# Vector arithmetic moved from GpSimd to VectorE in an encoder layer, with earlier first forms and a third early pair

## The chip, the cores and the metric

The kernel runs on one core of one Trainium2 chip. The metric is device time in microseconds (us). The core's engines work side by side, each through its own instruction stream in program order: TensorE (PE; its weight loads are shown as PEld), VectorE (DVE), ScalarE (ACT), GpSimd (POOL) and SyncE (SP). SP only issues DMAs; POOL issues some too. Engines wait for each other through semaphores.

## The reference

One layer of an encoder in float32: 512 tokens, model width 2048.

```python
h = rms_norm(x, g_mix_pre)
proj = h @ w_in                                   # 2048 x 6144
out_a = diff_attention(...)                       # heads 0 to 7
out_b = stick_breaking(...)                       # heads 8 to 15
mix = concatenate([out_a, out_b]) @ w_out         # 2048 x 2048
x = x + rms_norm(mix, g_mix_post)
h = rms_norm(x, g_mem_pre)
o = memory_attention(h, mem_n, w_mq, w_mkv, w_mo) # 4 heads, 256 memory tokens
x = x + rms_norm(o, g_mem_post)
h = rms_norm(x, g_ffn_pre)
gu = h @ w_gate_up                                # 2048 x 11264
f = (silu(gu[..., :D_FF]) * gu[..., D_FF:]) @ w_down
x = x + rms_norm(f, g_ffn_post)
```

## The kernel before, in words

**Precision.** A float32 product is made of three PE matmuls on parts: each operand is split into a rounded part h (a cast on ACT) and the rest l = x - h (a subtraction on DVE), and PE sums h*h, h*l and l*h. A weight of 128x1024 (512 KB) is split by `Weights.split`: L127 is the cast on ACT, L128 the subtraction on DVE. A 128x512 piece of activations is split by `split` (L236 cast, L237 subtraction). PE's matmuls nearly all come from the helper `mm` (L233).

**Weights.** All weights pass in one fixed list of chunks. `Weights.load` issues them on SP (L116) as slots come free: five slots `raws`, with three more (`mraw`, later `raw`) at some places. Some chunks are sums of two blocks of a weight. Those are made by a second, accumulating DMA that POOL issues: onto a fresh load (L118), or onto a slot whose chunk is already split (L136, "add"). Some are summed on DVE (L133). Two weights ahead of the one in use are split.

**Products.** The out-projection (`w_out`) and the FFN (`w_gu`, `w_dn`) are block products with seven products in place of eight, in class `Blocks`: columns in pairs of 512, tokens in two halves. Product i takes a *form* of the activations (a quarter, or a sum or difference of quarters, split in h and l) and a chunk for each of 4 blocks; it is 4 x 12 = 48 matmuls of 512 columns for a pair of columns. Forms are stored in quarters of the large tile `big`, or in tiles of their own. `evict` then adds the product in PSUM to what is held (L912, L973, L980; L1006 and L1007 for product 7 when it came before 6).

**Stages.** Cross-attention keys and values; 16 heads (0 to 7 differential, 8 to 15 stick-breaking), each with its projection; out-projection; cross-attention; FFN. Stick-breaking is a chain through ACT (e, sph, w, sqh), DVE and PE. Its results, with those of the other heads, are `mix`. The out-projection first makes product 1 and product 7 of both pairs (`EARLY`, from heads 0 to 7 alone), then 2, 3, 5, 6, 4 of each pair. After it, each of four token blocks t has a `chain`: residual (L844), transposes on PE (L854) and splits. Beside it PE folds the memory keys into `w_mq` (`fold_keys`). In the FFN products 1 and 2 of the first two column pairs are made *early*, before the forms of 5, 3, 6, 7 and 4 are needed (`late_forms`); L861 is the scaling of a transposed token block ahead of them.

**What sets the order.** Work that is to run beside PE's matmuls is written as generators in two queues, `side` and `side2`. `fill`, called behind every few matmuls, steps both: a generator yields an integer (so many steps) or a float (so many us of matmuls) to wait. A scheduler then orders each engine's instructions; an instruction that is pinned (`pin`, keep in program order) can't be moved ahead of its predecessor on its engine.

**What the change touches.** `sub_p` (L909) is a subtraction of 128x512 on POOL: 16 of them for the out-projection's forms (`mix_forms`), 16 for `late_forms`. L1006 and L1007 are 8 sums on POOL, L1079 a gain, on DVE for tokens of the first half and on POOL (8 times) for the second. `mix_form(1, 0)` makes the first form of product 1 once all heads are written down; the other three follow in `mix_forms` with `big` as home.

Of the kernel before, what the change touches and what calls it, by code (L numbers as in the profile page):

```python
# [36 lines left out]
NF = 12  # L37
NQ = 8
TW = 640

# [151 lines left out]
def encoder_kernel(ctx: ExitStack, tc: tile.TileContext, a: dict, out: bass.AP):  # L192
# [114 lines left out]
    for cb in range(NCB):  # L307
        wm("w_mo", cb, range(8))
    for j, cbs in enumerate(gu_cbs[:2]):
        wf("w_gu", cbs, 0, 4, ORDER[:2], MAKE)  # L310
    for j, cbs in enumerate(gu_cbs):
        wf("w_gu", cbs, 0, 4, ORDER[2 if j < 2 else 0 :], MAKE, j == 1)
    for b, n in enumerate(DOWN):
# [410 lines left out]
    def sb_gen(h, q, k, v):  # L724
# [52 lines left out]
        yield from subnorm(o, h, gains[:, G_SB : G_SB + 1])  # L777

    for g in range(4):
        v = v_block(g)  # L780
        for h in range(4 * g, 4 * g + 4):
            cq, ck = qk_cts(h)
            scale = 64 ** -0.5 if h < HD else 128 ** -0.5
            if h + 1 < HD:
                spread_bias(h + 1)
            q = proj_hl("w_qk", cq, scale)
            k = proj_hl("w_qk", ck, 1.0)
            side.add((diff_gen if h < HD else sb_gen)(h, q, k, v))


# [3 lines left out]
    class Sub:  # L794
# [78 lines left out]

        def chain(self, t):
            ss2 = yield from self.residual(t, True)
            yield CH[0]
            for cb in range(NCB):
                self.turn(t, cb)
                if cb == NCB - 1:
                    s2, r2 = st(), st()  # L880
                    nc.vector.tensor_reduce(s2, ss2, axis=AX.X, op=ALU.add)
                    pow_rstd(r2, s2, 1)
                    self.r2[t] = r2
                yield CH[1]
# [22 lines left out]

    def sub_p(o, x, y):
        nc.gpsimd.tensor_tensor(o, x, y, op=ALU.subtract)  # L909

    def sub2(o, x, y):
        nc.vector.tensor_tensor(o, x, y, op=ALU.subtract)  # L912

    class Blocks:
# [55 lines left out]
        def evict(self, i, t, p):  # L970
# [17 lines left out]
            elif i == 6:  # L988
# [13 lines left out]
                if (7, t) in T:  # L1002
                    w = T.pop((7, t))

                    def last():
                        nc.gpsimd.tensor_tensor(v, v, w, op=ALU.add)  # L1006
                        nc.gpsimd.tensor_tensor(r, r, w, op=ALU.add)  # L1007

# [14 lines left out]

    mixforms = {}

    def mix_form(i, k2, src, loose=False):
        if i in HOMES_MIX and not loose:
            a_, b_ = HOMES_MIX[i]
            k = 8 * a_ + 2 * k2
            h, l = (big[:, x, k : k + 2, b_ * M : (b_ + 1) * M] for x in range(2))  # L1030
        else:
            h, l = u2(s="mixh"), u2(s="mixl")
        split(h, l, src)
        mixforms[i, k2] = (h, l)

    def mix_forms():

        for k2 in range(1, 4):
            mix_form(1, k2, mix[k2, 0])
            yield 2  # L1040
        for k2 in range(4):
            t = u2(F32, "s7")
            sub_p(t, mix[k2, 1], mix[k2, 0])
            mix_form(7, k2, t)
            yield 2
        for k2 in range(4):
# [3 lines left out]
            mix_form(2, k2, a12)  # L1050
            sub_p(a21, a21, a22)
            yield 1
            sub_p(a11, a11, a21)
            yield 1
            sub_p(a12, a12, a11)
            late_mix[k2] = (a12, a21, a11, a22)
            yield 1
# [3 lines left out]
            yield 1  # L1061
        for n, i in enumerate((5, 6, 4)):
            for k2 in range(4):
                while (7, 1) not in done_mix:
                    yield 0
                mix_form(i, k2, late_mix[k2][1 + n])
                yield 2.0
# [6 lines left out]
    def mix_done(cbs):  # L1074
        def done(t, nh, c):
            cb = cbs[nh]
            sub.mark = c
            nc.scalar.activation(junk, c, AF.Square, accum_out=sub.ss[t][:, cb : cb + 1])
            (nc.vector if t < 2 else nc.gpsimd).tensor_tensor(c, c, sub.g[cb], op=ALU.mult)  # L1079
            sub.y[t, cb] = c  # L1080
            if cb == col_pairs[-1][t < 2]:
                (side, side2)[t // 2].add(sub.chain(t))
        return done
# [4 lines left out]

    mix_form(1, 0, mix[0, 0], True)
    side2.add(mix_forms())  # L1090
# [100 lines left out]
    for pair in range(2):  # L1191
        for r in range(KT):
            fold_keys(pair, r)
        if pair == 0:
            side2.add(load_keys(1))
        else:
            side2.add(load_values([0], True))
# [79 lines left out]
    def early_forms(t):  # L1277
        while not fv_done:
            yield 0
        for i, g0 in ((1, 0), (2, 2)):  # L1280
            for g in range(2):
                form(i, g, t, h3[g0 + g, t])
                yield 0

    def late_forms(t):
        for g in range(2):
            a11, a12, a21, a22 = (h3[g + 2 * c, t + 2 * r] for r in range(2) for c in range(2))
            s = u(s="s")
            sub_p(s, a21, a22)
            form(5, g, t, s)  # L1290
            yield 0
            sub_p(a21, a21, a11)
            form(7, g, t, a21)
            yield 0
            sub_p(s, a11, s)
            form(6, g, t, s)
            yield 0
            sub_p(a12, a12, s)
            form(3, g, t, a12)
            yield 0  # L1300
            form(4, g, t, a22)
            yield 0

# [155 lines left out]

    early = [Blocks("w_gu", cbs, 0, 4, gated(j)) for j, cbs in enumerate(gu_cbs[:2])]  # L1460
    for g in early:
# [7 lines left out]
    for j, cbs in enumerate(gu_cbs):  # L1469
        g = early[j] if j < 2 else Blocks("w_gu", cbs, 0, 4, gated(j))  # L1470
        past = set()
        if j == NFB - 1:
            side2.add(block_forms(0, past))
        for i in ORDER[2 if j < 2 else 0 :]:
            g.product(i)
# [146 lines left out]
```

## Time and profile before

| | us |
|---|---|
| runs of before: median (lowest, highest) of 3 | 2753.44 (2747.07, 2760.84) |
| the profiled execution | 2757.57 |
| its span, from first to last instruction | 2755.4 |
| POOL's subtractions at L909 (32), busy | 55.1 |
| POOL's powers of 128x1 at L388 (20), busy | 17.3 |

The profile is of one execution. A page gives busy time by engine, the span in 40 slices, and the costliest groups of instructions; a trace answers further questions: who waited for whom, instructions in order of time, and busy times by stretch. "Granted clock" is the share of full speed at which TensorE was let run.

### The profile page before, as it was taken

How to read it: one execution, taken by the hardware profiler on the slowest of the kernel's cores; microseconds unless marked ns; L12 is line 12 of the kernel's file. 1: busy time of each engine (PE TensorE's matmuls, PEld its weight loads, DVE VectorE, ACT ScalarE, POOL GpSimd, SP SyncE). 2: the span in 40 equal slices, each digit the busy share in tenths (PEclk: the TensorE clock that was granted, in tenths of full speed). 3: DMA queues.
4: the chain of work that ended last, by engine and by line, in shares of the span. 5: the costliest groups of instructions: out<-in, count | busy, mean ns of one | idle time of the engine just before them, and what ended most of it. 6: DMA issues, size and time to landing. Idle time of an engine off the chain costs nothing.

```text
span 2755.4 us, 33701 instructions
## 1 busy us (share of the span) xinstructions
PE 2663.9 (97%) x12608; PEld 2205.2 (80%) x12608; DVE 1717.0 (62%) x2329; ACT 1322.9 (48%) x1936; POOL 336.0 (12%) x345
## 2 busy tenths in 40 slices
PE   8999999999997998999998999999999999999996
PEld 7888877888886778888886888888888888878775
DVE  5673555554456779335467655555555568787887
ACT  5542444455455546334445444444444456454553
POOL 0000000000003132000015221111211221102101
PEclk9999999999998999999999999999999999999998
DMA  8882222222225776233556998888989889878776
GB/s 287 294 266 97 81 92 84 82 87 76 77 74 148 188 194 215 78 122 106 163 174 149 249 216 206 203 202 203 203 202 207 198 221 252 222 248 202 199 205 204
DMA packets 166021, 480.64 MB, mean 174 GB/s; under 512 B 18529, under 2 KB 29177, under 8 KB 165857
## 3 DMA queue, kind: packets, MB, share of 16 engines
q1 hardware_dynamic: 127776, 344.37, 37.1%
q0 software_dynamic: 38080, 134.12, 26.5%
q8 instruction: 98, 1.61, 0.2%
q14 instruction: 67, 0.54, 0.1%
HBM read 441.70 MB, written 39.34 MB: 175 GB/s over the span
## 4 chain that ended last, share of the span: by engine, by line
PE 82%; DMA 5%; issue 5%; DVE 5%; ACT 1%; POOL 1%; SPq 0%; POOLq 0%; ACTq 0%; DVEq 0%
PE ps L233 80%; DVE parts L128 2%; DMA raws<-in_w_dn_dram 1%; DMA xres<-x_d 1%; DMA mraw<-in_w_out_dram 1%; ACT parts L127 1%; PE ps L1368 1%; DMA kraw<-kT_d 1%; DVE big L237 1%; DMA actT_d<-fT 0%; POOL y_d L1488 0%; DMA raw<-in_w_dn_dram 0%; DMA xnat<-in_x_dram 0%; PE ps L854 0%; DVE form L237 0%
## 5 line engine op out<-in xcount | busy, mean ns | idle before, releaser
L233 PE MATMUL ps<-parts,big 128*128 128x512 f32 x4824 | 1141.0, 394 | 38.2 <-DVE parts L128 24.1
L233 PEld LDWEIGHTS ps<-parts,big 128*128 128x128 f32 x4824 | 907.2, 189 | 239.6 <-DVE parts L128 33.9
L128 DVE TENSOR_TENSOR parts<-raws,parts 128x1024 fp32r<-128x1024 f32 x555 | 686.9, 1240 | 572.7 <-ACT parts L127 567.6
L127 ACT CAST parts<-raws 128x1024 fp32r<-128x1024 f32 x555 | 583.1, 1052 | 704.3 <-PE ps L233 628.6
L233 PE MATMUL ps<-parts,form 128*128 128x512 f32 x2376 | 552.3, 390 | 2.9 <-ACT parts L127 2.7
L233 PEld LDWEIGHTS ps<-parts,form 128*128 128x128 f32 x2376 | 444.7, 188 | 97.7 <-ACT parts L127 4.8
L233 PE MATMUL ps<-big,parts 128*128 128x512 f32 x1536 | 375.2, 394 | 0.0
L233 PEld LDWEIGHTS ps<-big,parts 128*128 128x128 f32 x1536 | 282.7, 188 | 61.4 <-issue 3.9
L128 DVE TENSOR_TENSOR parts<-raw,parts 128x1024 fp32r<-128x1024 f32 x175 | 216.1, 1238 | 154.7 <-ACT parts L127 154.4
L127 ACT CAST parts<-raw 128x1024 fp32r<-128x1024 f32 x175 | 183.9, 1054 | 197.2 <-PE ps L233 161.0
L136 POOL DMA_DIRECT2D raws<-in_w_gu_dram x112 | 97.8, 873 | 823.2 <-DVE parts L128 622.8
L233 PE MATMUL ps<-memhl,parts 128*128 128x512 f32 (+1 forms) x1024 | 184.0, 341 | 10.4 <-DVE memhl L244 8.8
L233 PEld LDWEIGHTS ps<-memhl,parts 128*128 128x128 f32 x1024 | 158.1, 190 | 35.6 <-DVE memhl L244 8.8
L233 PE MATMUL ps<-khl,parts 128*128 128x256 f32 x768 | 99.3, 289 | 0.0
L233 PEld LDWEIGHTS ps<-khl,parts 128*128 128x128 f32 x768 | 95.5, 195 | 0.2
L118 POOL DMA_DIRECT2D raws<-in_w_out_dram x12 | 11.0, 920 | 686.0 <-DMA raws<-in_w_out_dram 680.1
L233 PE MATMUL ps<-big,pTh 128*128 128x512 f32 x256 | 80.1, 392 | 0.0
L233 PE MATMUL ps<-gh,big 128*128 128x512 f32 x256 | 79.1, 389 | 0.0
L136 POOL DMA_DIRECT2D raw<-in_w_gu_dram x60 | 52.4, 873 | 111.6 <-DVE parts L128 108.4
L688 ACT ACTIVATE e<-e,small 128x512 f32<-128x512 f32 (+3 forms) x64 | 35.4, 555 | 51.9 <-DVE small L686 51.9
L136 POOL DMA_DIRECT2D raws<-in_w_dn_dram x30 | 26.2, 875 | 256.5 <-DVE parts L128 203.8
L233 PEld LDWEIGHTS ps<-gh,big 128*128 128x128 f32 x256 | 48.1, 188 | 10.0
(964 smaller groups left out, 2381.3 us busy)
## 6 DMA issues: line engine op xcount, KB each, us to landing
raws<-in_w_gu_dram POOLq DMA_DIRECT2D x113, 512.0 KB, 6.7
raws<-in_w_gu_dram SPq DMA_DIRECT2D x79, 512.0 KB, 4.4
raws<-in_w_qk_dram SPq DMA_DIRECT2D x64, 512.0 KB, 3.3
raw<-in_w_gu_dram POOLq DMA_DIRECT2D x63, 512.0 KB, 6.8
raw<-in_w_gu_dram SPq DMA_DIRECT2D x57, 512.0 KB, 3.7
aq<-actT_d SPq DMA_DIRECT2D x82, 256.0 KB, 6.0
raws<-in_w_dn_dram SPq DMA_DIRECT2D x41, 512.0 KB, 5.4
raws<-in_w_mk_dram SPq DMA_DIRECT2D x32, 512.0 KB, 5.1
```

The source lines that it names most:

```text
L118: self.nc.gpsimd.dma_start(t[0], x, accum_op=ALU.add)
L127: self.nc.scalar.copy(h, r)
L128: self.nc.vector.tensor_tensor(l, r, h.bitcast(F32), op=ALU.subtract)
L136: self.nc.gpsimd.dma_start(r, self.chunks[m][3], accum_op=ALU.add)
L233: nc.tensor.matmul(o, l, r, start=start, stop=stop, skip_group_check=True)
L237: pin(nc.vector.tensor_tensor(l, src, h.bitcast(F32), op=ALU.subtract))
L688: nc.scalar.activation(es[m][:, 0:n], es[m][:, 0:n], AF.Exp, bias=nmx[:, m : m + 1], accum_out=z[:, m : m + 1],)
L1368: nc.tensor.transpose(tp[:, k * P : (k + 1) * P], f[:, k * P : (k + 1) * P], ident)
```

## The change

All tile arithmetic of `sub_p`, L1006, L1007 and L1079 is issued on VectorE. The two 128x512 adds of the last residual (L842) and the small powers stay on GpSimd. The first form of the out-projection is made for all four blocks by a generator that is queued with head 12, one piece per 12 us of matmuls, in tiles of its own. Forms of the out-projection and the FFN, and the subtractions ahead of them, are pinned. In `mix_forms` form 5 moves up to the first loop. The chains of token blocks 2 and 3 wait for 12 us of matmuls first. `load_keys(1)` goes to the other queue. A third column pair of the FFN has its products 1 and 2 early; the chunk of its product 5 is then loaded anew (four chunks) rather than summed in place.

```diff
+NE = 3
...
-    for j, cbs in enumerate(gu_cbs[:2]):
+    for cbs in gu_cbs[:NE]:
         wf("w_gu", cbs, 0, 4, ORDER[:2], MAKE)
     for j, cbs in enumerate(gu_cbs):
-        wf("w_gu", cbs, 0, 4, ORDER[2 if j < 2 else 0 :], MAKE, j == 1)
+        wf("w_gu", cbs, 0, 4, ORDER[2 if j < NE else 0 :], MAKE, 0 < j < NE)
...
+    def mix_form(i, k2, src, loose=False):
+        if i in HOMES_MIX and not loose:
...
+        split(h, l, src, pin)
+        mixforms[i, k2] = (h, l)
+
+    def first_forms():
+
+        for k2 in range(4):
+            mix_form(1, k2, mix[k2, 0], True)
+            yield 12.0
+
     for g in range(4):
...
+            if h == 12:
+                side2.add(first_forms())
...
-        def chain(self, t):
+        def chain(self, t, wait=0.0):
+            yield wait
...
-    def sub_p(o, x, y):
-        nc.gpsimd.tensor_tensor(o, x, y, op=ALU.subtract)
-
     def sub2(o, x, y):
-        nc.vector.tensor_tensor(o, x, y, op=ALU.subtract)
+        return nc.vector.tensor_tensor(o, x, y, op=ALU.subtract)
...
-                        nc.gpsimd.tensor_tensor(v, v, w, op=ALU.add)
-                        nc.gpsimd.tensor_tensor(r, r, w, op=ALU.add)
+                        add(v, v, w)
+                        add(r, r, w)
...
     def mix_forms():
-        for k2 in range(1, 4):
-            mix_form(1, k2, mix[k2, 0])
-            yield 2
         for k2 in range(4):
             t = u2(F32, "s7")
-            sub_p(t, mix[k2, 1], mix[k2, 0])
+            pin(sub2(t, mix[k2, 1], mix[k2, 0]))
             mix_form(7, k2, t)
...
             mix_form(3, k2, a12)
             yield 1
-        for n, i in enumerate((5, 6, 4)):
+            mix_form(5, k2, a21)
+            yield 1
+        for n, i in enumerate((6, 4)):
...
-            (nc.vector if t < 2 else nc.gpsimd).tensor_tensor(c, c, sub.g[cb], op=ALU.mult)
+            nc.vector.tensor_tensor(c, c, sub.g[cb], op=ALU.mult)
             sub.y[t, cb] = c
             if cb == col_pairs[-1][t < 2]:
-                (side, side2)[t // 2].add(sub.chain(t))
+                (side, side2)[t // 2].add(sub.chain(t, 12.0 * (t > 1)))
...
-    mix_form(1, 0, mix[0, 0], True)
+    side2.drain()
     side2.add(mix_forms())
...
-            side2.add(load_keys(1))
+            side.add(load_keys(1))
...
     def late_forms(t):
...
-            sub_p(s, a21, a22)
-            form(5, g, t, s)
-            yield 0
+            pin(sub2(s, a21, a22))
+            form(5, g, t, s, 4, pin)
+            yield 3.0
...
-    early = [Blocks("w_gu", cbs, 0, 4, gated(j)) for j, cbs in enumerate(gu_cbs[:2])]
+    early = [Blocks("w_gu", cbs, 0, 4, gated(j)) for j, cbs in enumerate(gu_cbs[:NE])]
```

How it moves instructions, at three places. First POOL, from the loads of the out-projection on (`mix` and `s` are the operands of the forms, `raws` and `mraw` the weights' slots). Before:

```order
L118 DMA raws<-in_w_out_dram 128x1024 x5
L909 TENSOR_TENSOR s_816_6704<-mix_2460,mix_2458 128x512
L909 TENSOR_TENSOR s_820_6745<-mix_3111,mix_3109 128x512
L909 TENSOR_TENSOR mix_2460<-mix_2460,mix_5026 128x512
L909 TENSOR_TENSOR mix_3111<-mix_3111,mix_5562 128x512
L118 DMA raws<-in_w_out_dram 128x1024
L909 TENSOR_TENSOR mix_2458<-mix_2458,mix_2460 128x512
```

Of the change:

```order
L120 DMA raws<-in_w_out_dram 128x1024 x9
L120 DMA mraw_7041<-in_w_out_dram 128x1024
L120 DMA mraw_7042<-in_w_out_dram 128x1024
L120 DMA raws<-in_w_out_dram 128x1024
L138 DMA raws<-in_w_out_dram 128x1024 x3
```

POOL's stream there holds accumulating loads alone; the subtractions that stood between them are gone from it.

Second PE, in the stick-breaking chain of head 14 (`sph`, `spl` are its two parts, `mixh`, `mixl` those of product 1's form). Before:

```order
L233 MATMUL ps_6445<-spl_6474,nones_r 128x256
L233 MATMUL ps_6444<-sph_6482,ntri_r 128x384
L233 MATMUL ps_6444<-sph_6473,nones_r 128x256 x2
L233 MATMUL ps_6444<-spl_6483,ntri_r 128x384
L233 MATMUL ps_6444<-spl_6474,nones_r 128x256 x2
L233 MATMUL ps_6443<-sph_6491,ntri_r 128x512
```

Of the change:

```order
L235 MATMUL ps_6461<-spl_6490,nones_r 128x256
L235 MATMUL ps_6568<-parts,mixh_5912 128x512 x2
L235 MATMUL ps_6568<-parts,mixl_5913 128x512
L235 MATMUL ps_6569<-parts,mixh_5912 128x512 x2
L235 MATMUL ps_6569<-parts,mixl_5913 128x512
L235 MATMUL ps_6568<-parts,mixh_5912 128x512
L235 MATMUL ps_6460<-sph_6498,ntri_r 128x384
L235 MATMUL ps_6460<-sph_6489,nones_r 128x256 x2
L235 MATMUL ps_6460<-spl_6499,ntri_r 128x384
```

Matmuls of product 1 now stand between the steps of the chain: 7 here, 22 ahead of the step of 128x512.

Third DVE, while the late forms of the FFN are made (`h` and `s` are the operands, `form` and `big` the results, `parts` the weights). Before:

```order
L128 TENSOR_TENSOR parts<-raw_10876,parts 128x1024
L237 TENSOR_TENSOR big<-s_11172,big 128x4x128
L237 TENSOR_TENSOR form_11115<-h_1208_10991,form_11114 128x512
L128 TENSOR_TENSOR parts<-raw_10877,parts 128x1024
L237 TENSOR_TENSOR form_11120<-h_1210_10998,form_11119 128x512
```

Of the change:

```order
L130 TENSOR_TENSOR parts<-raw_10883,parts 128x1024
L932 TENSOR_TENSOR s_11111<-h_1180_10673,s_11111 128x512
L239 TENSOR_TENSOR form_11145<-h_1218_11009,form_11144 128x512
L932 TENSOR_TENSOR h_1220_11016<-h_1220_11016,h_1196_10785 128x512
L239 TENSOR_TENSOR big<-s_11115,big 128x4x128
L130 TENSOR_TENSOR parts<-raws,parts 128x1024
```

The subtractions stand in DVE's stream now, between the weight splits; with the third pair 8 more weight splits stand in this stretch.

More of the change, by code (lines that the diff above doesn't have):

```diff
@@ L777, in sb_gen @@
         yield from subnorm(o, h, gains[:, G_SB : G_SB + 1])
+    mixforms = {}
+    def mix_form(i, k2, src, loose=False):
+        if i in HOMES_MIX and not loose:
+            a_, b_ = HOMES_MIX[i]
+            k = 8 * a_ + 2 * k2
+            h, l = (big[:, x, k : k + 2, b_ * M : (b_ + 1) * M] for x in range(2))
+        else:
+            h, l = u2(s="mixh"), u2(s="mixl")
+        split(h, l, src, pin)
[4 more added lines that the diff above has]
+            yield 12.0
     for g in range(4):
@@ L1021, in evict @@
                 later.append(lambda: self.done(2 + t, 0, r))
[L1024 to L1034, printed above, removed]
     def mix_forms():
-        for k2 in range(1, 4):
-            mix_form(1, k2, mix[k2, 0])
-            yield 2
         for k2 in range(4):
             t = u2(F32, "s7")
-            sub_p(t, mix[k2, 1], mix[k2, 0])
+            pin(sub2(t, mix[k2, 1], mix[k2, 0]))
             mix_form(7, k2, t)
@@ L1050, in mix_forms @@
             mix_form(2, k2, a12)
-            sub_p(a21, a21, a22)
+            pin(sub2(a21, a21, a22))
             yield 1
-            sub_p(a11, a11, a21)
+            pin(sub2(a11, a11, a21))
             yield 1
-            sub_p(a12, a12, a11)
-            late_mix[k2] = (a12, a21, a11, a22)
+            pin(sub2(a12, a12, a11))
+            late_mix[k2] = (a11, a22)
             yield 1
@@ L1065, in mix_forms @@
                     yield 0
-                mix_form(i, k2, late_mix[k2][1 + n])
+                mix_form(i, k2, late_mix[k2][n])
                 yield 2.0
@@ L1281, in early_forms @@
             for g in range(2):
-                form(i, g, t, h3[g0 + g, t])
+                form(i, g, t, h3[g0 + g, t], 4, pin)
                 yield 0
@@ L1288, in late_forms @@
             s = u(s="s")
-            sub_p(s, a21, a22)
-            form(5, g, t, s)
-            yield 0
[L1292 to L1302, printed above, removed]
+            pin(sub2(s, a21, a22))
+            form(5, g, t, s, 4, pin)
+            yield 3.0
+            pin(sub2(a21, a21, a11))
+            form(7, g, t, a21, 4, pin)
+            yield 3.0
+            pin(sub2(s, a11, s))
+            form(6, g, t, s, 4, pin)
+            yield 3.0
+            pin(sub2(a12, a12, s))
+            form(3, g, t, a12, 4, pin)
+            yield 3.0
+            form(4, g, t, a22, 4, pin)
+            yield 3.0
     def cross_out(cb, toks, accs):
@@ L1469, in encoder_kernel @@
     for j, cbs in enumerate(gu_cbs):
-        g = early[j] if j < 2 else Blocks("w_gu", cbs, 0, 4, gated(j))
+        g = early[j] if j < NE else Blocks("w_gu", cbs, 0, 4, gated(j))
         past = set()
@@ L1473, in encoder_kernel @@
             side2.add(block_forms(0, past))
-        for i in ORDER[2 if j < 2 else 0 :]:
+        for i in ORDER[2 if j < NE else 0 :]:
             g.product(i)
```

## The prediction

> **What bounds the kernel now.** I read the head of the page first, then stretches of 25 us side by side, then who TensorE waited for.
>
> ```profile
> span 2755.4 us, 33701 instructions
> PE 2663.9 (97%) x12608; PEld 2205.2 (80%) x12608; DVE 1717.0 (62%) x2329; ACT 1322.9 (48%) x1936; POOL 336.0 (12%) x345
> ...
> PE   8999999999997998999998999999999999999996
> ...
> PEclk9999999999998999999999999999999999999998
> ```
>
> TensorE (PE) is busy for 97% of the span, and the change takes no matmul away, so only its 91.5 us of idle time (2755.4 - 2663.9), and time lost to a lower clock, can be won. The slices show dips at slices 13 to 16 (826 to 1102 us: last heads, out-projection, first cross-attention folds), slice 22 (1446 to 1515: start of the FFN), and at both ends. The change touches only the two inner places. The stretches there (us, then per engine busy us and instructions, the granted PE clock, DMA share, GB/s):
>
> ```profile
> 828.00:850.00 22.00, 19.54 (x89) 16.26 (x88) 10.94 (x14) 14.47 (x23) 1.84 (x2) 0.92 0.37 99
> 850.00:875.00 25.00, 17.32 (x72) 13.40 (x71) 18.55 (x13) 10.69 (x16) 14.31 (x13) 0.82 0.97 228
> 875.00:900.00 25.00, 18.39 (x72) 14.81 (x72) 20.80 (x22) 14.72 (x27) 8.22 (x6) 0.77 0.38 105
> ...
> 925.00:950.00 25.00, 19.91 (x77) 15.28 (x76) 19.88 (x21) 11.80 (x17) 2.76 (x3) 0.86 0.56 142
> 950.00:975.00 25.00, 23.85 (x105) 19.11 (x104) 20.14 (x18) 14.16 (x21) 13.55 (x9) 1.00 0.70 167
> 975.00:1000.00 25.00, 22.11 (x89) 17.29 (x88) 19.97 (x21) 9.84 (x15) 8.13 (x7) 0.93 0.80 189
> 1000.00:1025.00 25.00, 24.48 (x107) 19.65 (x106) 12.63 (x23) 11.25 (x17) 3.42 (x4) 1.00 0.91 245
> 1025.00:1050.00 25.00, 19.98 (x95) 15.99 (x95) 21.17 (x28) 12.18 (x23) 8.75 (x6) 0.86 0.52 167
> 1050.00:1075.00 25.00, 17.15 (x126) 16.98 (x125) 23.85 (x44) 17.92 (x41) 10.82 (x9) 0.80 0.81 286
> ...
> 1450.00:1475.00 25.00, 16.37 (x60) 11.71 (x58) 25.00 (x18) 14.95 (x22) 22.24 (x12) 0.93 0.29 101
> 1475.00:1500.00 25.00, 24.78 (x108) 20.27 (x109) 17.38 (x20) 12.50 (x16) 6.40 (x8) 1.00 0.83 179
> 1500.00:1525.00 25.00, 25.00 (x112) 20.68 (x111) 15.69 (x17) 11.09 (x12) 6.68 (x8) 1.00 0.99 215
> ```
>
> A full stretch holds 112 matmuls of 512 columns (1500 to 1525), 0.223 us each. I take as lost the idle time plus busy time x (1 - clock). That gives 4.0 + 10.8 + 10.8 = 25.6 for 828 to 900, 7.9 for 925 to 950, 1.2 + 4.4 = 5.6 for 950 to 1000, 0.5 + 7.8 = 8.3 for 1000 to 1050 and 11.3 for 1050 to 1075: 58.7 us. From 1450 to 1500 it is 9.8 + 0.2 = 10.0. In all **68.7 us** is in reach. Who PE waited for, 825 to 1080 (four rows) and 1420 to 1480 (the last): total us, times, longest.
>
> ```profile
> PE ps L233 <- DVE parts L128: 16.3, 9, 4.3
> PE ps L854 <- DVE p__807_6674 L844: 7.9, 1, 7.9
> PE ps L233 <- DVE big L237: 5.7, 1, 5.7
> PE ps L233 <- ACT sph L236: 3.6, 3, 1.8
> ```
> ```profile
> PE ps L233 <- DVE parts L128: 8.8, 5, 3.4
> ```
>
> VectorE (DVE) ends nearly all of it. Yet in most of these stretches DVE is busy for only 20 of 25 us, so I looked at how long its instructions take. First 863 to 870 (start, us, engine), then groups (count, busy us, mean ns, then the idle time before them) of 860 to 890, of 1425 to 1475, and of the undisturbed FFN, 1500 to 2300:
>
> ```profile
> 863.78 6.91 DVE L237 TENSOR_TENSOR big<-s,big 128x512 fp32r<-128x512 f32 x1 [2.30 <-ACT big L236]
> ...
> 863.96 2.82 POOL L909 TENSOR_TENSOR mix<-mix,mix 128x512 f32<-128x512 f32 x2
> ...
> 867.03 3.11 POOL L909 TENSOR_TENSOR mix<-mix,mix 128x512 f32<-128x512 f32 x2
> ```
> ```profile
> L237 DVE TENSOR_TENSOR big<-s,big 128x512 fp32r<-128x512 f32 x2 | 9.8, 4886 | 2.3 <-ACT big L236 2.3
> L128 DVE TENSOR_TENSOR parts<-raws,parts 128x1024 fp32r<-128x1024 f32 x4 | 9.1, 2264 | 2.2 <-ACT parts L127 2.2
> L237 DVE TENSOR_TENSOR big<-mix,big 128x512 fp32r<-128x512 f32 x4 | 3.7, 949 | 0.0
> ```
> ```profile
> L237 DVE TENSOR_TENSOR form<-h,form 128x512 fp32r<-128x512 f32 x8 | 11.2, 1428 | 0.0
> L128 DVE TENSOR_TENSOR parts<-raw,parts 128x1024 fp32r<-128x1024 f32 x7 | 11.2, 1595 | 0.5 <-ACT parts L127 0.5
> L237 DVE TENSOR_TENSOR big<-s,big 128x512 fp32r<-128x512 f32 x5 | 8.2, 1648 | 0.0
> L128 DVE TENSOR_TENSOR parts<-raws,parts 128x1024 fp32r<-128x1024 f32 x4 | 6.7, 1666 | 0.0
> ...
> L861 DVE TENSOR_TENSOR h<-ps,small 128x512 f32<-128x512 f32 x8 | 5.3, 685 | 0.8 <-PE ps L854 0.7
> ```
> ```profile
> L128 DVE TENSOR_TENSOR parts<-raws,parts 128x1024 fp32r<-128x1024 f32 x180 | 219.7, 1224 | 199.8 <-ACT parts L127 199.8
> ...
> L1410 DVE TENSOR_TENSOR aq<-aq,aq 128x512 f32<-128x512 f32 x11 | 7.5, 685 | 0.0
> ```
>
> One form split took 6.91 us instead of 0.68, and GpSimd (POOL) ran subtractions for nearly all of it. The excess of the quoted groups is 2 x 4.20 + 4 x 1.04 + 4 x 0.26 = 13.6 us in 860 to 890, and 8 x 0.74 + 7 x 0.37 + 5 x 0.96 + 4 x 0.44 = 15.1 us in 1425 to 1475. POOL's DMA issues are no cause: POOL is 6.68 us busy in 1500 to 1525, and the splits still take 1224 ns.
>
> [...] The sum below goes by the rows.
>
> **The change part by part.**
>
> *All 48 subtractions, sums and gains of 128x512 from POOL to DVE*: 32 at L909, 8 at L1006/L1007, 8 at L1079. Each costs DVE 0.685 us (L1410, same shape), 32.9 us in all. In 860 to 890 there are 13: 8.9 us added against 13.6 freed. In 1425 to 1475 there are 16: 11.0 against 15.1. So DVE gets lighter where it is the bound, and the links of the form chain shrink from some 1.5 us to 0.7. POOL's queue holds only DMAs and the small powers, so accumulating loads are not issued behind arithmetic.
>
> *First forms during heads 12 to 15*: the same 4 ACT casts and 4 DVE splits, in stretches where DVE has room. Before, three of the four had to wait for `big`. Now 96 matmuls of product 1 (21.4 us) can stand between the steps of head 14's chain, as the order shows. With both: 828 to 900 loses 25.6 now. I leave the 3.6 us of waits on ACT sph (a chain through ACT and DVE that nothing shortens) and 1 us of clock: **-21**.
>
> *900 to 950.* What is late next is the last head. In the new order DVE has 21 instructions of 0.685 and 11 of 1.22 us between that head's last product and product 4's first form, 27.8 us, for 7 weights, which PE eats in 7 x 12 x 0.223 = 18.7 us. So 9 us could be waited for, from 0 if the work starts early. I take 7 of today's 7.9: **-1**.
>
> *950 to 1050.* Splits of product 5 and 4 wait for weights that are accumulated by DMA, at these landing times (841 to 887, then 1005 to 1030):
>
> ```profile
> raws<-in_w_out_dram SPq DMA_DIRECT2D x10, 512.0 KB, 3.4
> raws<-in_w_out_dram POOLq DMA_DIRECT2D x8, 512.0 KB, 7.0
> ```
> ```profile
> raws<-in_w_out_dram POOLq DMA_DIRECT2D x3, 512.0 KB, 8.6
> ```
>
> These transfers stay. What goes is the part that DVE adds behind them. I take **-3.5** of 5.6 (POOL's four gains stood ahead of two accumulating loads) and **-4** of 8.3. Bounds: 0 and 13.9.
>
> *1050 to 1075*: PE stood 7.9 us before a transpose of token block 2, whose residual had been queued behind the others. The chains of blocks 2 and 3 now start 12 us later, and 120 matmuls of the key fold stand in between. What stays is POOL's power of 128x1, which still slows a residual beside it:
>
> ```profile
> L844 DVE SCALAR_TENSOR_TENSOR c__864_7133<-c__864_7133,small,xres 128x512 f32<-128x512 f32 x1 | 1.8, 1771 | 0.4 <-POOL small L388 0.4
> ```
>
> Eight of 1.1 us excess could stay; I leave 3.3 of 11.3: **-8**.
>
> *Third early pair and forms in program order (1450 to 1500)*: PE gets 96 more matmuls, 21.4 us, before it needs the late forms, and DVE 8 weight splits (9.8 us) with them, which are moved, not added. **-8.5** of 10.0. Pair 2's product 5 now needs four loads of 512 KB that it had as an in-place sum. Their slots come free earlier in exchange. The landing time above, 3.4 us, makes that 0 to 13.6; I take 0, because PE did not wait at a DMA share of 0.99.
>
> Sum: 21 + 1 + 3.5 + 4 + 8 + 8.5 = 46. The profiled execution took 2757.6 us (2.2 around its span), 4.1 above the median of the runs. 2757.6 - 46 - 4.1 = **2708**.
>
> [...] Here 828 to 850 fell to 0.92 with no wait over 1.8. [...]
>
> **The rivals.**
>
> *Weights become the bound in 828 to 900.* A product-7 weight needs a load and an accumulating load, 10.4 us by the medians. Five slots at 12 matmuls each give 13.4 us, so it just fits, without reserve. If PE, freed of the forms, runs into it at 1.6 us for each of 8 weights, 13 us of the 21 stay: 2721. For: a DMA share of 0.97 in 850 to 875. Against: PE's small matmuls of head 15 stretch the time. Chance 0.19.
>
> *The stall moves.* The new order fixes forms among weight splits. If a form or the last head comes late, all splits behind it do. Then of the 46 only the 21 of 828 to 900 are won, and the 27.8 against 18.7 us at the last head (9) comes on top of today's waits, since PE now gets there earlier: 2753.4 - 21 + 9 = 2741. For: DVE is busy for 23.85 of 25 us in 1050 to 1075 already. Against: freed of POOL it has room there. Chance 0.09.
>
> *DVE becomes the bound.* It takes 32.9 us more, and in 1450 to 1475 it is busy for 25.00 of 25. If the long DVE instructions had another cause than POOL's arithmetic, the 16 there (11.0) come on top in full, and a third of the 32 others (7.3): 2753.4 + 18 = 2772 with nothing won elsewhere. It turns slower once less than 70% of the excess goes (32.9 against some 47 us over the whole run, estimated from 28.7 for the 29 subtractions of the two groups). Against: the excess is only where POOL computes. [...] Chance 0.05.
>
> That nothing is moved is excluded: the order of POOL has none of the 48 left.
>
> **How the numbers follow.** Forecast 0.67, rivals 0.19, 0.09, 0.05. The range goes from all 68.7 won (2757.6 - 68.7 - 4.1 = 2685) to 2740, between the second rival and the third. 0.5% is 13.8 us, about what a measurement tells from no change: faster means under 2739.7. Forecast and first rival lie there, 0.86; same 0.09; slower 0.05.
>
> **What would show it.** DVE's weight splits at 1.22 us and form splits at 0.69 in every stretch; DVE's total busy time not above 1717 in spite of 48 more instructions; no wait of PE over 4 us between 828 and 900 and clock above 0.9 there; a wait of some us on `big` or `parts` where the last head ends; full stretches from 1450. Wrong would be: splits still at 1.6 us or more, PE waiting in 830 to 900 on splits that wait for a DMA, or new waits after 1500 from the four loads.

## The result

| us | before | changed |
|---|---|---|
| median of 4 runs | 2754.15 | 2713.69 |
| lowest, highest | 2747.07, 2760.84 | 2708.29, 2714.11 |
| profiled execution | 2757.57 | 2713.29 |

The ratio is 0.9849, 95% interval 0.9821 to 0.9877: 40.5 us less. The forecast was 2708, with a range from 2685 to 2740. The head of the page of the changed kernel, with the slices that answer to those of before:

```profile
span 2711.3 us, 33699 instructions
PE 2647.8 (98%) x12608; PEld 2193.1 (81%) x12608; DVE 1697.6 (63%) x2377; ACT 1322.3 (49%) x1936; POOL 253.1 (9%) x297
...
PE   8999999999999889999999999999999999999996
...
PEclk9999999999999999999999999999999999999998
```

DVE runs 48 instructions more (2377 against 2329) and is busy for 19.4 us less. Since the 48 cost 32.9 us by the prediction's 0.685 us each, 52.3 us of slowing are gone over the whole run (the estimate was 47). The dips at slices 13, 16 and 22 are gone; slices 14 and 15 show a shallow one. The same stretches (columns as before):

```profile
825.00:850.00 25.00, 25.00 (x126) 21.25 (x125) 16.46 (x20) 17.33 (x26) 3.57 (x4) 1.00 0.64 171
850.00:875.00 25.00, 24.16 (x114) 19.61 (x114) 17.39 (x24) 16.76 (x27) 3.48 (x4) 1.00 0.99 253
875.00:900.00 25.00, 21.64 (x94) 16.27 (x93) 21.67 (x33) 19.23 (x30) 1.75 (x2) 1.00 0.73 224
900.00:925.00 25.00, 18.58 (x70) 13.09 (x70) 19.90 (x25) 11.01 (x18) 1.75 (x2) 0.93 0.49 114
...
1000.00:1025.00 25.00, 19.27 (x93) 14.88 (x92) 19.68 (x34) 11.51 (x18) 1.48 (x1) 0.93 0.66 194
...
1050.00:1075.00 25.00, 21.79 (x161) 21.21 (x162) 20.72 (x31) 15.50 (x29) 2.15 (x2) 0.93 0.60 208
...
1450.00:1475.00 25.00, 24.90 (x111) 20.28 (x110) 19.57 (x24) 14.53 (x20) 4.35 (x5) 1.00 0.79 194
```

Lost time, counted as in the prediction: 825 to 900 loses 0.8 + 3.4 = 4.2 us (before 25.6). 900 to 925 loses 6.4 idle + 1.3 by the clock = 7.7 (before, 925 to 950, 7.9). 1000 to 1025 loses 5.7 + 1.3 = 7.1, and 1450 to 1475 only 0.1 (before 9.8). DVE's groups in 820 to 900 (the first two) and in 1425 to 1475 (the others) show why:

```profile
L130 DVE TENSOR_TENSOR parts<-raws,parts 128x1024 fp32r<-128x1024 f32 x20 | 24.4, 1222 | 15.2 <-ACT parts L129 14.9
...
L239 DVE TENSOR_TENSOR big<-s,big 128x512 fp32r<-128x512 f32 x4 | 2.7, 684 | 0.2 <-ACT big L238 0.2
```
```profile
L130 DVE TENSOR_TENSOR parts<-raw,parts 128x1024 fp32r<-128x1024 f32 x11 | 13.4, 1216 | 2.3 <-ACT parts L129 2.3
...
L239 DVE TENSOR_TENSOR form<-h,form 128x512 fp32r<-128x512 f32 x12 | 8.0, 680 | 0.0
```

These splits are back at their undisturbed length: 684 ns where the mean was 4886, 1222 where it was 2264. What PE still waits for in 820 to 1075 (total us, times, longest):

```profile
PE ps L235 <- DVE parts L130: 10.0, 11, 3.6
PE ps L235 <- ACT parts L129: 6.5, 4, 3.0
PE ps L235 <- DVE big L239: 3.7, 4, 2.5
```

`parts` are weights: PE now waits mostly for their casts (L129) and splits (L130). The longest wait for a split has its cause in DVE's rows from 904 (start, us, then the idle time before it):

```profile
904.40 1.23 DVE L135 TENSOR_TENSOR raws<-raws,mraw 128x1024 f32<-128x1024 f32 x1 [2.15 <-DMA mraw<-in_w_out_dram]
905.54 1.22 DVE L130 TENSOR_TENSOR parts<-raws,parts 128x1024 fp32r<-128x1024 f32 x1
```

DVE stands for 2.15 us at a sum of two weights (L135) that waits for a transfer; the split behind it, for which PE waited 3.6 us, follows at once. The longest wait for a cast ends at 1003.2. ACT's rows there:

```profile
1001.52 0.71 ACT L238 CAST khl<-kraw 128x256 fp32r<-128x256 f32 x2 [7.76 <-DMA kraw<-kT_d]
1002.14 1.04 ACT L129 CAST parts<-raws 128x1024 fp32r<-128x1024 f32 x1
```

ACT stands for 7.76 us at a cast of the memory keys (`load_keys`), whose transfer is late, and the weight's cast is queued behind it.

### The profile page after: what moved, and what is told of

Its sections match the earlier page's. It is cut to its first block, busy times and chain, and to the rows that moved or that the text cites. A ratio compares the mean times of both kernels' runs of the same rounds, so it can differ in the third digit from the quotient of the medians.

```text
span 2711.3 us, 33699 instructions
## 1 busy us (share of the span) xinstructions
PE 2647.8 (98%) x12608; PEld 2193.1 (81%) x12608; DVE 1697.6 (63%) x2377; ACT 1322.3 (49%) x1936; POOL 253.1 (9%) x297
## 4 chain that ended last, share of the span: by engine, by line
PE 82%; DMA 6%; issue 6%; DVE 4%; POOL 1%; ACT 1%; SPq 0%; POOLq 0%; DVEq 0%; ACTq 0%
PE ps L235 81%; DMA raws<-in_w_out_dram 1%; DVE parts L130 1%; DMA aq<-actT_d 1%; PE ps L1375 1%; DMA kraw<-kT_d 1%; DMA xnat<-in_x_dram 1%; ACT parts L129 1%; DMA raw<-in_w_dn_dram 0%; PE ps L876 0%; POOL y_d L1495 0%; PE ps L713 0%; POOL raws L138 0%; DVE big L239 0%; DMA y_d<-p__1711_18451 0%
## 5 line engine op out<-in xcount | busy, mean ns | idle before, releaser
L235 PE MATMUL ps<-parts,big 128*128 128x512 f32 x4752 | 1113.6, 391 | 20.7 <-DVE parts L130 10.2
L235 PEld LDWEIGHTS ps<-parts,big 128*128 128x128 f32 x4752 | 886.8, 188 | 216.9 <-DVE parts L130 18.2
L130 DVE TENSOR_TENSOR parts<-raws,parts 128x1024 fp32r<-128x1024 f32 x552 | 673.4, 1223 | 558.5 <-ACT parts L129 551.0
L129 ACT CAST parts<-raws 128x1024 fp32r<-128x1024 f32 x552 | 580.3, 1053 | 701.7 <-PE ps L235 617.3
L130 DVE TENSOR_TENSOR parts<-raw,parts 128x1024 fp32r<-128x1024 f32 x178 | 217.1, 1222 | 151.4 <-ACT parts L129 150.1
L129 ACT CAST parts<-raw 128x1024 fp32r<-128x1024 f32 x178 | 187.1, 1054 | 200.9 <-PE ps L235 165.1
L235 PEld LDWEIGHTS ps<-big,pTh 128*128 128x128 f32 x256 | 47.4, 188 | 9.5
```

Source lines behind the costliest of these rows:

```text
L129: self.nc.scalar.copy(h, r)
L130: self.nc.vector.tensor_tensor(l, r, h.bitcast(F32), op=ALU.subtract)
L235: nc.tensor.matmul(o, l, r, start=start, stop=stop, skip_group_check=True)
```

## The experiments

To set runs beside each other I take the time between marks that all kernels have, from one profile each: A, from the last projection of the heads to the last product of the out-projection; B, from there to the end of the key fold; D, the FFN up to its last transposed activations; E, the rest to the last product. Between B and D, cross-attention takes 224.7 us in each of these kernels.

| kernel | median | ratio to before (95%) | A | B | D | E |
|---|---|---|---|---|---|---|
| before | 2754.15 | 1 | 216.3 | 155.0 | 886.6 | 422.9 |
| changed | 2713.69 | 0.9849 (0.9821 to 0.9877) | 193.4 | 151.6 | 873.4 | 421.1 |
| move_only | 2726.93 | 0.9897 (0.9883 to 0.9911) | 192.1 | 156.7 | 879.2 | 424.5 |
| pool_back | 2726.89 | 0.9897 (0.9883 to 0.9911) | 201.1 | 148.0 | 879.3 | 421.6 |
| late_first_form | 2733.51 | 0.9922 (0.9909 to 0.9934) | 209.6 | 151.3 | 873.7 | 423.3 |
| two_pairs | 2714.87 | 0.9849 (0.9835 to 0.9863) | 193.0 | 152.8 | 874.4 | 424.0 |
| no_pins | 2720.67 | 0.9870 (0.9849 to 0.9891) | 190.7 | 152.8 | 878.6 | 425.8 |
| no_chain_wait | 2721.22 | 0.9875 (0.9858 to 0.9892) | 190.0 | 155.0 | 873.0 | 424.7 |
| apart_6_4 | 2712.75 | 0.9849 (0.9830 to 0.9868) | 189.3 | 154.0 | 873.0 | 425.0 |
| late_first_unpinned | 2715.09 | 0.9855 (0.9830 to 0.9880) | 194.5 | 151.5 | 873.7 | 421.7 |
| ffn_pins_only | 2714.21 | 0.9852 (0.9834 to 0.9870) | 191.4 | 151.5 | 873.7 | 424.3 |
| apart_later | 2710.33 | 0.9838 (0.9820 to 0.9856) | 188.2 | 148.9 | 873.4 | 426.1 |

E holds nothing that differs between most of these kernels, and still goes from 421 to 426; A of three kernels that are the same up to there (changed, two_pairs and the first probe below) is 193.4, 193.0 and 190.7. Differences of less than 3 us in one column are not read.

### The arithmetic alone, and the order alone

move_only is the kernel before with this:

```diff
-        nc.gpsimd.tensor_tensor(o, x, y, op=ALU.subtract)
+        nc.vector.tensor_tensor(o, x, y, op=ALU.subtract)
...
-                        nc.gpsimd.tensor_tensor(v, v, w, op=ALU.add)
-                        nc.gpsimd.tensor_tensor(r, r, w, op=ALU.add)
+                        nc.vector.tensor_tensor(v, v, w, op=ALU.add)
+                        nc.vector.tensor_tensor(r, r, w, op=ALU.add)
...
-            (nc.vector if t < 2 else nc.gpsimd).tensor_tensor(c, c, sub.g[cb], op=ALU.mult)
+            nc.vector.tensor_tensor(c, c, sub.g[cb], op=ALU.mult)
```

> The kernel before, with all 48 of GpSimd's 128x512 operations on VectorE and nothing else of the change. Theory A (GpSimd's arithmetic slowed VectorE's operations, and that made TensorE wait): most of the gain, 2715 to 2732 us; splits of 128x512 at 0.69 us and of 128x1024 at 1.22 us in every stretch. Theory B (the gain comes from the order: first forms during the heads, pins, third early pair): 2748 to 2765 us, no gain, since VectorE gets 32.9 us more to do.

pool_back is the changed kernel with the same lines the other way; its subtractions stay pinned, on GpSimd:

```diff
+    def sub_p(o, x, y):
+        return nc.gpsimd.tensor_tensor(o, x, y, op=ALU.subtract)
...
-            pin(sub2(a21, a21, a22))
+            pin(sub_p(a21, a21, a22))
```

> The changed kernel with the 48 operations on GpSimd again, and all of its new order kept (its subtractions pinned as before). Theory A: most of the gain is lost, 2735 to 2752 us, and DVE splits of several us stand beside GpSimd's operations again. Theory B: 2712 to 2722 us.

Theory A called move_only right, at 2727. For pool_back both theories were wrong: it also took 2727, between their ranges. So each half gives some 28 us alone, and both give 40: they overlap. The columns say where. In A the arithmetic alone gives all of it (192.1), the order alone two thirds (201.1). In B the order gives all and more (148.0; why this is 3.6 us below the changed kernel was not followed), the arithmetic nothing (156.7). In D each gives 7 us, both 13.

Of the arithmetic's part, DVE's groups of move_only in 860 to 890 are proof: the work is written in the order of before, and the splits that took 4886 ns on average take 684. Over the whole run DVE is busy for 1698.8 us in move_only, where the changed kernel has 1697.6 and pool_back, with 48 instructions fewer, 1708.5.

```profile
L128 DVE TENSOR_TENSOR parts<-raws,parts 128x1024 fp32r<-128x1024 f32 x8 | 9.8, 1223 | 2.3 <-ACT parts L127 2.3
...
L237 DVE TENSOR_TENSOR big<-s,big 128x512 fp32r<-128x512 f32 x4 | 2.7, 684 | 0.0
```

What move_only lacks in B is seen in whom PE waited for from 1014 to 1073:

```profile
PE ps L854 <- DVE p__807_6674 L844: 9.0, 1, 9.0
```

That is the transpose of before, which waited 7.9 us. With GpSimd's gains gone, the wait is still there.

### The early first form, and the pins

late_first_form makes the first form of product 1 as the kernel before does:

```diff
-            if h == 12:
-                side2.add(first_forms())
...
     def mix_forms():
+        for k2 in range(1, 4):
+            mix_form(1, k2, mix[k2, 0])
+            yield 2
...
-    side2.drain()
+    mix_form(1, 0, mix[0, 0], True)
     side2.add(mix_forms())
```

> The changed kernel with the first form of the out-projection made as before: its first piece once all heads are written down, the other three by mix_forms, in big. Theory A: little is lost, 2714 to 2720 us, as the three pieces are made at full speed. Theory B: the dip of 828 to 900 comes back in part, 2724 to 2738 us.

Theory B called this one, at 2733.5, and the kernel is slower than the one that only moves the arithmetic (192.1 in A against 209.6). The stall sits later than in the kernel before: 13.28 us of PE in 25 at 900, and the clock at 0.69. The stretch, and whom PE waited for there:

```profile
900.00:925.00 25.00, 13.28 (x39) 8.78 (x38) 17.64 (x24) 8.60 (x13) 3.50 (x4) 0.69 0.74 199
```
```profile
PE ps L235 <- ACT big L238: 9.6, 2, 4.9
```

PE waits there twice for forms. The first wait, 4.7 us, ends with forms that need the last head's results, written from 906.5 on. Ahead of the second, 4.9 us, the forms wait on DVE, which stands for 3.83 us at a sum of two weights whose load is late; the pinned subtractions (L930) are queued behind it:

```profile
918.72 1.23 DVE L135 TENSOR_TENSOR mraw<-mraw,raws 128x1024 f32<-128x1024 f32 x1 [3.83 <-DMA raws<-in_w_out_dram]
919.86 1.41 DVE L930 TENSOR_TENSOR mix<-mix,mix 128x512 f32<-128x512 f32 x2
```

Two more kernels ask whether the pins made the early form necessary. no_pins removes all new pins from the changed kernel (`free` hands back its argument):

```diff
-        split(h, l, src, pin)
+        split(h, l, src)
...
-            pin(sub2(a21, a21, a22))
+            free(sub2(a21, a21, a22))
...
-            form(5, g, t, s, 4, pin)
+            form(5, g, t, s)
```

> The changed kernel without the new pins on forms and on the subtractions ahead of them. Theory P (the fixed order keeps late forms from standing ahead of weight splits, and so helps): 2718 to 2728 us. Theory Q (the pins only tie forms to the wrong places; without the early first forms they were part of the stall at the last head): 2705 to 2712 us. No part of it if 2712 to 2716 us.

Theory P held in the FFN: D goes from 873.4 to 878.6, and PE waits near 1450 again (2.5 and 2.0 us, where the changed kernel waits for nothing from 1380 to 1520):

```profile
PE ps L235 <- DVE parts L130: 2.5, 3, 1.7
PE ps L235 <- ACT parts L129: 2.0, 1, 2.0
```

In A the pins give nothing (190.7). So the last two kernels of this group keep the FFN's pins and drop those of the out-projection, one of them with the late first form as well:

> The changed kernel with the first form of the out-projection made as before, and without pins on the out-projection's forms; the FFN's stay pinned. Theory S (the early first form is worth much only because the out-projection's forms are pinned): the time to the end of the out-projection is that of the kernel with only the arithmetic moved, 192 us from the last projection of the heads instead of 210, and the whole takes 2712 to 2719 us. Theory F (early first forms win by themselves): 2725 to 2734 us, as with the pins.

> The changed kernel without pins on the out-projection's forms; first forms early, the FFN's pins kept. Theory S: 2709 to 2715 us, and no wait near 1450 us; so the pins of the FFN carry all of the 7 us that the kernel without any new pins lost. If the out-projection's pins help: 2716 to 2722 us.

Theory S held in both: A is 194.5 and 191.4, as with the arithmetic alone, and D stays at 873.7. The early first form is worth 16 us when the out-projection's forms are pinned, and nothing that these runs show when they are not (3.1 us in A, from one profile each, and 0.9 in the medians). With the first form late, the pins cost 15 us in A (209.6 against 194.5).

### The third pair, and the chains

two_pairs sets `NE = 2` in the changed kernel.

> The changed kernel with two early column pairs in place of three. Theory A: 2711 to 2717 us, since the late forms are made in time once VectorE is undisturbed (no wait of TensorE between 1400 and 1500). Theory B: the 8.5 us of the late forms come back, 2720 to 2725 us, with waits on parts near 1450.

It took 2714.9, and PE waits for 0.7 us from 1400 to 1500: the third pair is not needed once DVE is undisturbed and the forms are in order.

no_chain_wait undoes the delay of the chains and, with it, the move of `load_keys(1)` to the other queue; which of the two matters was not tested apart:

```diff
-                (side, side2)[t // 2].add(sub.chain(t, 12.0 * (t > 1)))
+                (side, side2)[t // 2].add(sub.chain(t))
...
-            side.add(load_keys(1))
+            side2.add(load_keys(1))
```

> The changed kernel with the chains of token blocks 2 and 3 not held back, and the second pair's keys in the queue where they were. The kernel with only the arithmetic moved still waits 9.0 us for one transpose's residual near 1030 us, and the one with only the new order waits nowhere near it. Theory R (the order of the chains, not GpSimd, made that wait): 2718 to 2724 us, with one wait of TensorE of 5 to 9 us on a residual. Theory A (GpSimd's gains and power made it): 2712 to 2716 us and no such wait.

Theory R held: the wait for one residual comes back, and B goes from 151.6 to 155.0. Whom PE waited for from 1015 to 1072:

```profile
PE ps L876 <- DVE p__816_6692 L866: 6.9, 1, 6.9
```

The median lost 7.5 us; 3.4 of it show in B, and A gained as much as runs of one kernel differ.

### What is left: a wait near 1003 us

The next two expectations take the 3.0 us near 1003 for the wait on a weight that lands late. apart_6_4 takes the products of the second column pair in another order, so that product 4's accumulating load gets 10 us more:

```diff
+ORDERS_MIX = ORDER_MIX, (3, 5, 6, 2, 4)
...
-        for i in ORDER_MIX:
+        for i in ORDERS_MIX[n]:
...
-            if cb == col_pairs[-1][t < 2]:
+            if cb == col_pairs[-1][0]:
```

> The changed kernel with the second column pair of the out-projection in the order 3, 5, 6, 2, 4, so that product 4's accumulating load has another 10 us before TensorE comes to it; the chains of blocks 0 and 1 start with product 2, 10 us later. Theory W (weights that land late make the waits near 1003 us): these waits (3.0 + 0.5 + 0.3 us, and the lower clock) go, 2706 to 2711 us. Theory A: the waits stay as they are, 2712 to 2716 us, or more where the later chains are waited for.

A miss: 2712.75, no difference. The wait on a weight's cast is still there and still 3.0 us, now at 994, and block 0's residual, which starts later, is waited for. PE's waits in 985 to 1080, and ACT's row ahead of 994:

```profile
PE ps L877 <- DVE c__869_7143 L867: 6.0, 1, 6.0
PE ps L236 <- ACT parts L130: 3.0, 1, 3.0
```
```profile
992.54 0.40 ACT L239 CAST khl<-kraw 128x256 fp32r<-128x256 f32 x1 [8.64 <-DMA kraw<-kT_d]
```

ACT stands at a cast of the keys once more. The keys' loads are queued with product 5, which moved, and the wait moved with them; 10 us more for the accumulating load changed nothing. So Theory W falls. The landing times of the changed kernel say the same. Its loads issued from 987.6 to 988.4, with the us to landing:

```profile
raws<-in_w_out_dram POOLq DMA_DIRECT2D x1, 512.0 KB, 9.2
kraw<-kT_d SPq DMA_DIRECT2D x1, 256.0 KB, 13.8
```

The first is the accumulating load of the weight that PE waits for at 1003. It was issued at 987.75 and landed at 996.9, so the weight had lain there for 5.2 us when its cast began at 1002.1, behind the casts of the keys, whose load landed at 1001.5. A kernel with the keys loaded earlier was not tried.

apart_later keeps the order of apart_6_4 and holds back the chain of block 0: the chain waits are `(10.0, 0.0, 16.0, 12.0)[t]`, and the pins on the out-projection's forms are gone.

> As before it (no pins on the out-projection's forms), with products 6 and 4 of the second pair apart, and the chain of token block 0 held back by 10 us of matmuls, that of block 2 by 16. The kernel with only 6 and 4 apart traded the waits near 1003 us for one of 6.0 us on block 0's residual. If only that residual's place in TensorE's order cost it: 2704 to 2710 us and no wait over 2 us between 985 and 1080. If another wait takes its place: 2711 to 2717 us.

2710.33, the lowest median of all, but above the range that was expected, and its interval overlaps that of the changed kernel. The residual's wait is gone; of 985 to 1080 the wait behind the keys (3.3 us) and one on `big` (2.6 us) are left.

A and B are 7.9 us shorter than in the changed kernel, and E 5 longer, in a part where nothing was changed. Whether it beats the changed kernel is open.

### What a GpSimd operation costs VectorE

Two kernels add GpSimd operations on a scratch tile to the changed kernel, in the FFN's first product. The first has subtractions, each on the result of the one before it, then scalings, then powers, and at the end subtractions in groups of four:

```diff
+        two = lambda: pin(nc.gpsimd.tensor_tensor(y, y, x, op=ALU.subtract))
+        one = lambda: pin(nc.gpsimd.tensor_scalar(y, x, 2.0, None, op0=ALU.mult))
+        power = lambda: pin(nc.gpsimd.tensor_tensor(y[:, 0:1], x[:, 0:1], mhalf[:, 0:1], op=ALU.pow))
+        for op, n, gap in ((two, 1, 6.0), (one, 1, 6.0), (power, 1, 6.0), (two, 4, 12.0)):
```

> The changed kernel with 64 GpSimd operations on a scratch tile added in the FFN's first product, where VectorE has room: 16 subtractions of 128x512 one at a time, 16 scalings of 128x512 (one input), 16 powers of 128x1, and 16 subtractions in groups of four. Theory A: beside the subtractions splits of 1.22 us become 1.6 us and more, and in the groups of four some take 4 us or more (one operation shut out by several); powers of 128x1 slow a VectorE operation by up to 1.1 us; the time is the changed kernel's or up to 10 us more. If an operation of VectorE loses one GpSimd operation at most, none takes over 1.22 + 1.5 = 2.7 us, in the groups too.

DVE's splits of `raws` in its stretches of subtractions (1635 to 1720), scalings (1750 to 1845) and powers (1868 to 1970):

```profile
L130 DVE TENSOR_TENSOR parts<-raws,parts 128x1024 fp32r<-128x1024 f32 x20 | 30.3, 1515 | 18.6 <-ACT parts L129 17.2 <-DMA raw<-in_w_gu_dram 1.5
...
L130 DVE TENSOR_TENSOR parts<-raws,parts 128x1024 fp32r<-128x1024 f32 x23 | 30.1, 1309 | 26.6 <-ACT parts L129 26.4
...
L130 DVE TENSOR_TENSOR parts<-raws,parts 128x1024 fp32r<-128x1024 f32 x22 | 26.9, 1224 | 27.9 <-ACT parts L129 26.3 <-DMA raws<-in_w_gu_dram 1.5
```

In the first stretch DVE's operations took 10.4 us longer than their usual time (31 splits 7.6, two others 2.8), 0.7 for each of the 16 single subtractions. Beside the 16 scalings it was 3.2 us, 0.2 each, and beside the 16 powers nothing at all: the splits keep 1224 ns. None took over 2.65 us, in the groups of four neither. So the powers were wrongly suspected, and no group held a split for 4 us. The longest two beside one row of dependent subtractions, DVE first and POOL second:

```profile
2035.27 2.06 DVE L130 TENSOR_TENSOR parts<-raw,parts 128x1024 fp32r<-128x1024 f32 x1 [1.55 <-ACT parts L129]
2037.51 2.05 DVE L130 TENSOR_TENSOR parts<-raw,parts 128x1024 fp32r<-128x1024 f32 x1 [0.18 <-ACT parts L129]
```
```profile
2031.02 9.70 POOL L1480 TENSOR_TENSOR scr<-scr 128x512 f32<-128x512 f32 x5
```

But before had 6.91 us. The second kernel's subtractions therefore do not depend on their neighbour (128x352, so that the tiles fit):

```diff
+        def sub_to(k):
+            pin(nc.gpsimd.tensor_tensor(scr[:, 1 + k % 2], scr[:, 0], scr[:, 0], op=ALU.subtract))
```

> As the first probe, but the subtractions (128x352 here) don't depend on the one before them, so GpSimd can start one while the last still runs: 8 groups of four, then 4 groups of eight. If an operation of VectorE can be shut out by a row of GpSimd operations that follow without a gap, as the 6.91 us of before suggest, some take 4 us and more here, up to a whole group. If it loses one at most, as with the dependent ones (longest 2.65 us), none takes over 2.7 us.

One split took 10.21 us beside a row of GpSimd operations (both engines and PE, in order of time):

```profile
1775.70 10.21 DVE L130 TENSOR_TENSOR parts<-raws,parts 128x1024 fp32r<-128x1024 f32 x1 [1.36 <-ACT parts L129]
1776.26 8.55 POOL L1479 TENSOR_TENSOR scr<-scr 128x352 f32<-128x352 f32 x11
1785.83 1.21 DVE L130 TENSOR_TENSOR parts<-raw,parts 128x1024 fp32r<-128x1024 f32 x1
...
1785.96 2.50 PE L235 MATMUL ps<-parts,form 128*128 128x512 f32 x5 [5.47 <-DVE parts L130]
```

The 64 subtractions of this run take 1115 ns each on average, 71.4 us in all, and POOL is busy with them for 53.6 us, with no idle time ahead of them: they overlap. (In the first probe the 32 take 1833 ns each, and POOL is busy with them for all of these 58.7 us, with 1.4 us of idle time ahead of them.) The row ended at 1784.8 and the split at 1785.9, 1.1 us later, and PE waited 5.5 us. The split behind it took 1.21. The row of before at 863.78 looks the same, with one difference: there the issue of a load fills the 0.25 us between its second and third subtraction. Another split of before ended while POOL's row still ran:

```profile
879.22 5.41 DVE L128 TENSOR_TENSOR parts<-raws,parts 128x1024 fp32r<-128x1024 f32 x1 [0.59 <-ACT parts L127]
```

Three overlapping subtractions ran beside this split up to 883.53, the next began at 883.61, 0.08 us later, and the split ended at 884.6, while the row went on to 887.3. The whole time of this one run, 2754.5, isn't read: parts far from the added operations were longer too (cross-attention 228.1 us in place of 224.7).

## Why the prediction was right, point by point

**The bound.** It said that DVE ends PE's waits, that GpSimd's arithmetic makes DVE slow, and that moving it frees more than it costs. move_only shows it: 28 us from the move alone, with the splits of 860 to 890 at 684 and 1223 ns.

**828 to 900, -21.** It came out at 21.4 (25.6 to 4.2). The reason was half wrong: "With both", it said, the move and the early first form. Over all of A the move alone does as much. In the stretch itself the early form does win: move_only loses 8.5 us there. The waits on `sph`, 3.4 us in move_only, are gone from the changed kernel, though the prediction left them in as a chain "that nothing shortens": product 1's matmuls stand between its steps. But from 900 to 950 the changed kernel loses 7.9 us where move_only loses 5.2. The sum counted the pins on the out-projection's forms at nothing. They cost 15 us in A when the first form is late, and the early form made up for them; that the term held is in part luck.

**The second rival.** Its mechanism, forms fixed in the order that come late and hold up what stands behind them, is what late_first_form shows (A 16 us longer, a granted clock of 0.69 from 900 to 925). The early first form kept it out of the changed kernel.

**900 to 950, -1.** 7.9 became 7.7. The wait at the last head was foreseen between 0 and 9.

**950 to 1050, -3.5 and -4.** The stretches 950 to 1000 and 1000 to 1025 of the changed kernel lose 10.2 us, where 950 to 1050 lost 13.9: 3.7 won in place of 7.5. The two stretches up to 1000, not shown above:

```profile
950.00:975.00 25.00, 23.73 (x105) 19.31 (x105) 19.84 (x25) 13.51 (x21) 3.50 (x4) 1.00 0.84 206
975.00:1000.00 25.00, 23.17 (x101) 18.39 (x99) 12.76 (x21) 9.37 (x14) 3.50 (x4) 1.00 0.74 210
```

The step that failed is "Splits of product 5 and 4 wait for weights that are accumulated by DMA". Near 1003 the weight's load has landed, and its cast waits behind casts of the keys on ACT, and did so before as well: ACT's rows of before show the same idle time.

```profile
1021.51 0.71 ACT L236 CAST khl<-kraw 128x256 fp32r<-128x256 f32 x2 [5.35 <-DMA kraw<-kT_d]
1022.13 1.05 ACT L127 CAST parts<-raws 128x1024 fp32r<-128x1024 f32 x1
...
1027.18 0.40 ACT L236 CAST khl<-kraw 128x256 fp32r<-128x256 f32 x1 [4.00 <-DMA kraw<-kT_d]
```

In before, PE was still at work until 1023.2 and waited only behind the second of these, 1.5 us; in the changed kernel it comes earlier and waits 3.0 us behind the first. Of the first rival, weights as the bound, little is seen: at 904 and 909 DVE stands for 2.15 and 2.04 us at sums of weights.

**1050 to 1075, -8.** Lost time from 1025 to 1075 is now 5.3 us (0.5 + 4.7) against 11.3 before: 6.0. The mechanism was right in one half: without the chains' 12 us and the move of the keys' load, the wait comes back (no_chain_wait). The other half, "What stays is POOL's power of 128x1, which still slows a residual beside it", is the step that failed. In the probe a power costs 0.0 us, and two gains at L1079 stood beside the quoted residual of 1771 ns. Before's own rows have both, a split at full speed beside a power and the residual beside the gains:

```profile
1054.25 1.21 DVE L128 TENSOR_TENSOR parts<-raws,parts 128x1024 fp32r<-128x1024 f32 x1
1054.40 1.46 POOL L388 TENSOR_TENSOR small<-small 128x1 f32<-128x1 f32 x1 [0.38 <-DVE small L387]
...
1055.84 1.28 POOL L1079 TENSOR_TENSOR p__831_6816<-p__831_6816,gpost 128x512 f32<-128x512 f32 x1
1055.90 1.77 DVE L844 SCALAR_TENSOR_TENSOR c__864_7133<-c__864_7133,small,xres 128x512 f32<-128x512 f32 x1 [0.38 <-POOL small L388]
1057.08 1.72 POOL L1079 TENSOR_TENSOR p__832_6818<-p__832_6818,gpost 128x512 f32<-128x512 f32 x1
```

Nine weight splits of before run beside a power, and each takes 1.21 to 1.23 us. With the gains moved, the longest residual of this stage takes 0.75 us. What stays there are waits on other things (2.5 us on `big`, 1.3 on `gl`) and 1.5 us of clock.

**1450 to 1500, -8.5.** It came out at 9.9. Of its two reasons the third pair was the wrong one: by the runs, the move gives 7.4 us in D, the pins 5.2 on top of it, and the pair nothing that can be measured. The four added loads cost nothing that shows.

**The sum.** The terms measured are 21.4 + 0.2 + 3.7 + 6.0 + 9.9 = 41.2, against 46. The profiles differ by 44.3 us: another 2.4 were won before 828 (the last projection ends at 825.4 in place of 827.8), and 1.8 in E, where runs of unchanged code differ by as much. By the marks A and B are 26.3 us shorter, where the four terms there add up to 31.3, and D is 13.2 shorter, where its term is 9.9: lost time, as counted here, is some 5 us too much in the one and 3 too little in the other. That the sum comes so near the whole is luck to that extent.

**The 6.91 us.** The sum took the 2 x 4.20 us of excess at the two form splits as POOL's in full, and they are gone: such splits take 684 ns in the changed kernel. How much one operation can lose differs between the probes: beside dependent subtractions none took over 2.65 us, beside a row of 11 overlapping ones a split of 1.2 us took 10.21. A scaling, with one input, cost 0.2 us where a subtraction, with two, cost 0.7.

**The clock.** The prediction left 1 us of clock in 828 to 900, where none was lost: the three stretches from 825 to 900 are at 1.00. Elsewhere it was lost after short waits. In the changed kernel, after waits of 3.6, 3.0 and 2.5 us (with another of 1.3 shortly before the last), the granted clock was 0.50 from 908.2 to 911.6, from 1003.8 to 1007.2 and from 1055.0 to 1058.4. The three stretches at 0.93 lose 4.1 us by it.

## What to carry to other kernels

Group an engine's common instruction by stretch and look for long durations: VectorE, at 62% busy, was the bound where its operations were stretched (4886 ns for 684). Price a move between engines with the freed time as well as the added; here 32.9 us of work took 52.3 us of slowing away. Test the parts of a change one by one and in pairs: two halves that give 28 us each gave 40 together, and one part only repaired what another had cost. For a wait, look at what the in-order engine itself stood at just before: a late key load was behind what read as a late weight. Before an operation is blamed, look in the same trace for others beside it: nine splits beside powers, all at full speed, were there from the start.

## What the runs showed that was not expected

Beside a row of 11 independent, overlapping GpSimd subtractions a VectorE split of 1.2 us took 10.21 us; beside subtractions of which each depends on the one before, no operation took over 2.65. A scaling with one input cost 0.2 us on average, a power of 128x1 nothing. Pinned forms cost some 15 us in the out-projection when the first form was late, and won 5 in the FFN. In before and in the changed kernel weights that had landed lay for 4 to 6 us (4.0 and 6.0 before, 5.2 in the changed kernel) near the end of the out-projection, because their casts stood on ScalarE behind that of another, late load.
